# Loads and stores of two pairs issued as runs of four transfers

## The chip, the cores and the metric

One core of a Trainium2 chip. The metric is the device time of the whole kernel in microseconds (us); less is better. All comparisons here are between fast runs on one chip at a time. A ratio is the mean time of one kernel's fast runs over that of the kernel before in the same rounds, so it is not quite the ratio of the medians that stand beside it. Names of engines: PE is TensorE's matmuls and PEld its weight loads, DVE is VectorE, ACT ScalarE, POOL GpSimd; SP is SyncE, which here only issues transfers.

## The reference

`x` is [64, 1024, 1024] in fp32, 268 MB; the output has the same shape. Each token (row of 1024) goes to one of 16 heads, the one with the largest routing logit, and only that head's 64 columns of the output are not zero.

```python
route_logits = x @ route_w                      # [B, S, 16]
best_head = np.argmax(route_logits, axis=-1)
x_heads = x.reshape(B, S, 16, 64)
for h in range(16):
    out[:, :, h, :] = np.matmul(x_heads[:, :, h, :], experts[h]) * (best_head == h)[:, :, None]
```

## The kernel before

A *pair* is two tiles of 128 tokens, 1 MB of input and 1 MB of output; there are 256 pairs. A pair is loaded by two transfers of 512 KB (even and odd partitions) and stored by two. SP issues them all, on one queue, in the order load, load, store, store. Each transfer is spread over 16 DMA engines: four packets of 8 KB on each, then a write to a semaphore.

```python
WAYS = 2; XIN_BUFS = 10; OUT_BUFS = 6; XT_BUFS = 5; AHEAD = 7
ORDER = "TTTTFTFTFTTFTFTFTTTTTT"      # T: transpose on TensorE, F: matmul of a whole block

def load(g):
    xin = xin_pool.tile([P, 2, D], FP32, name="xin", tag="xin")
    for r in range(WAYS):
        nc.sync.dma_start(out=xin[r::WAYS], in_=xg[g, r::WAYS])
    return xin

def split_pass(xt):                   # five of eight blocks, in 64x64 parts of the array
    ps = ps_s_pool.tile([P, 2, HB], FP32, name="ps_s", tag="ps_s")
    for p in range(NS):
        ...
        for half in range(2):
            for th in range(2):
                nc.tensor.matmul(ps[th * 64:(th + 1) * 64, half, o0:o0 + W],
                    lhsT=xt[half * 64:(half + 1) * 64, p, th * 64:(th + 1) * 64],
                    rhs=mv[half * 64:(half + 1) * 64, p, :], ...)
    ...                               # ACT copies ps to raw, DVE sums logits

for j in range(-2 * AHEAD, NT + 2, 2):          # j: first tile of a pair
    if j + 2 * AHEAD < NT:
        xins[j + 2 * AHEAD] = load(j // 2 + AHEAD)
    if j < 0:
        continue
    pair = [i for i in (j - 2, j - 1) if i >= 0]
    for i in pair:
        work[i] = split_pass(xts[i])            # at the start of the pair's period
    ...                                         # then T of pair j, F of pair j-2, by ORDER
                finish(ot[:, i % 2, :], ps_w, *work.pop(i))   # argmax, mask; DVE and POOL write ot
                if i == pair[1]:
                    for r in range(WAYS):
                        nc.sync.dma_start(out=og[i // 2, r::WAYS], in_=ot[r::WAYS])
```

The split pass of a pair is recorded as 80 small matmuls and takes TensorE about 1.54 us of the 4.93 us that it needs for a pair.

## Time and profile before

| | before |
|---|---|
| time, median of 3 runs | 1341.66 us (1338.74 to 1343.21) |
| span of the profiled run | 1338.1 us |
| TensorE's period of a pair, median / mean | 4.926 / 5.136 us |
| one 8 KB packet, undisturbed | 309 ns |

The page of the kernel before: busy time of the compute engines, the busy share of the DMA engines and the data rate in forty slices of the span, the queue with its packets, MB and share of the 16 engines, and the chain of waits by engine and by line.

```profile
span 1338.1 us, 66342 instructions
...
PE 1290.3 (96%) x27648; PEld 1208.3 (90%) x27648; DVE 933.7 (70%) x4098; ACT 923.2 (69%) x1537; POOL 721.9 (54%) x1031
...
DMA  8999999999999999999999999999999999999997
GB/s 340 421 421 416 413 407 409 407 407 406 412 398 377 418 417 399 395 412 414 398 393 404 410 416 418 402 408 397 410 407 410 412 407 417 416 405 416 417 409 327
...
q1 hardware_dynamic: 81920, 536.94, 98.6%
...
HBM read 268.76 MB, written 268.44 MB: 401 GB/s over the span
...
DMA 96%; PE 1%; SPq 0%; DVE 0%; issue 0%; POOL 0%; ACT 0%; ACTq 0%; POOLq 0%; DVEq 0%
DMA out_dram<-ot 95%; DMA xin<-in_x_dram 1%; SPq L106 0%; PE ps_w L150 0%; PE ps_t L115 0%; DMA mv<-in_route_w_dram 0%; PE ps_s L136 0%; POOL ot L181 0%; DVE ot L173 0%; ACTq L88 0%; ACT raw L143 0%; ACT xt L117 0%; DVE mask L164 0%; POOLq L249 0%; DVE lg L158 0%
```

Nearly the whole span is filled by the one DMA queue, and the chain runs through stores. TensorE at 96% is close behind, which is why its pair period is worth reading: the median of 4.926 us is a pair without a wait, and the mean is 0.21 us longer.

Three stretches of the same run. Columns: stretch, its length, then busy us of each engine with its number of instructions, TensorE's granted clock, DMA share, GB/s.

```profile
core 0: us, PE busy (x) PEld busy (x) DVE busy (x) ACT busy (x) POOL busy (x), PEclk, DMA share, GB/s
600.00:650.00 50.00, 49.82 (x1083) 46.98 (x1083) 36.40 (x160) 36.04 (x61) 27.85 (x41) 1.00 1.01 411
650.00:700.00 50.00, 49.00 (x1077) 46.24 (x1076) 35.63 (x159) 35.32 (x60) 27.47 (x41) 1.00 1.00 392
1100.00:1200.00 100.00, 98.86 (x2142) 91.57 (x2141) 71.84 (x311) 70.29 (x118) 54.69 (x78) 1.00 1.01 412
```

The DMA share is 1.00 in all of them.

Who waits for whom, three lines of that view:

```profile
engine line waited for: us in total, times, longest us
...
DVE ot L173 <- DMA out_dram<-ot: 83.8, 104, 1.8
...
POOL ot L181 <- DMA out_dram<-ot: 76.3, 40, 3.0
...
PE ps_t L115 <- DMA xin<-in_x_dram: 6.9, 2, 6.6
```

Compute waits for stores to give back an output buffer, and hardly ever for a load. SP's own order of issues (start, duration, line, out<-in, count):

```profile
start us, us, engine line op out<-in xcount [idle before <-releaser]
602.66 0.50 SPq L223 DMA_DIRECT2D out_dram<-ot  x1
603.92 1.68 SPq L106 DMA_DIRECT2D xin<-in_x_dram  x2
606.49 1.77 SPq L223 DMA_DIRECT2D out_dram<-ot  x2
```

Each issue waits for the landing of the eighth transfer before, so eight are outstanding.

### The profile page before, as it was taken

How to read it: one execution, taken by the hardware profiler on the slowest of the kernel's cores; microseconds unless marked ns; L12 is line 12 of the kernel's file. 1: busy time of each engine (PE TensorE's matmuls, PEld its weight loads, DVE VectorE, ACT ScalarE, POOL GpSimd, SP SyncE). 2: the span in 40 equal slices, each digit the busy share in tenths (PEclk: the TensorE clock that was granted, in tenths of full speed). 3: DMA queues.
4: the chain of work that ended last, by engine and by line, in shares of the span. 5: the costliest groups of instructions: out<-in, count | busy, mean ns of one | idle time of the engine just before them, and what ended most of it. 6: DMA issues, size and time to landing. Idle time of an engine off the chain costs nothing.

```text
span 1338.1 us, 66342 instructions
## 1 busy us (share of the span) xinstructions
PE 1290.3 (96%) x27648; PEld 1208.3 (90%) x27648; DVE 933.7 (70%) x4098; ACT 923.2 (69%) x1537; POOL 721.9 (54%) x1031
## 2 busy tenths in 40 slices
PE   7999999999999999999999999999999999999995
PEld 7888998999998999999998999889998999999995
DVE  4666766677776777777777677667777777767775
ACT  5666766767766777777676776667766767767673
POOL 3455555555555555555555555555555555555554
PEclk9999999999999999999999999999999999999998
DMA  8999999999999999999999999999999999999997
GB/s 340 421 421 416 413 407 409 407 407 406 412 398 377 418 417 399 395 412 414 398 393 404 410 416 418 402 408 397 410 407 410 412 407 417 416 405 416 417 409 327
DMA packets 84412, 541.51 MB, mean 405 GB/s; under 512 B 18576, under 2 KB 18576, under 8 KB 18576
## 3 DMA queue, kind: packets, MB, share of 16 engines
q1 hardware_dynamic: 81920, 536.94, 98.6%
q8 instruction: 218, 3.57, 1.0%
q10 hardware_dynamic: 2192, 0.33, 0.1%
q14 instruction: 82, 0.67, 0.1%
HBM read 268.76 MB, written 268.44 MB: 401 GB/s over the span
## 4 chain that ended last, share of the span: by engine, by line
DMA 96%; PE 1%; SPq 0%; DVE 0%; issue 0%; POOL 0%; ACT 0%; ACTq 0%; POOLq 0%; DVEq 0%
DMA out_dram<-ot 95%; DMA xin<-in_x_dram 1%; SPq L106 0%; PE ps_w L150 0%; PE ps_t L115 0%; DMA mv<-in_route_w_dram 0%; PE ps_s L136 0%; POOL ot L181 0%; DVE ot L173 0%; ACTq L88 0%; ACT raw L143 0%; ACT xt L117 0%; DVE mask L164 0%; POOLq L249 0%; DVE lg L158 0%
## 5 line engine op out<-in xcount | busy, mean ns | idle before, releaser
L181 POOL TENSOR_TENSOR ot<-raw,mask 128x384 f32<-128x384 f32 (+1 forms) x1024 | 721.2, 725 | 605.6 <-ACT xt L117 338.0
L117 ACT COPY xt<-ps_t 128x512 f32<-128x512 f32 x1024 | 576.7, 589 | 288.5 <-PE ps_t L115 288.0
L115 PE MATMUL ps_t<-ident,xin 128*128 128x128 f32 x4096 | 756.5, 277 | 9.7 <-DMA xin<-in_x_dram 6.9
L150 PE MATMUL ps_w<-mf,xt 128*128 128x144 f32 x3072 | 580.3, 289 | 1.5 <-DVE ot L173 1.1
L115 PEld LDWEIGHTS ps_t<-ident,xin 128*128 128x128 f32 x4096 | 499.7, 141 | 33.6 <-issue 8.9
L150 PEld LDWEIGHTS ps_w<-mf,xt 128*128 128x128 f32 x3072 | 464.2, 191 | 8.8 <-DVE ot L173 6.3
L136 PE MATMUL ps_s<-mv,xt 64*64 64x80 f32 x20480 | 430.0, 232 | 22.6 <-issue 21.9
L136 PEld LDWEIGHTS ps_s<-mv,xt 64*64 64x64 f32 x20480 | 381.1, 133 | 73.2 <-issue 62.8
L143 ACT COPY raw<-ps_s 128x704 f32<-128x704 f32 x512 | 371.1, 747 | 104.3 <-PE ps_s L136 64.9
L173 DVE TENSOR_TENSOR ot<-ps_w,mask 128x384 f32<-128x384 f32 x512 | 285.6, 558 | 98.5 <-DMA out_dram<-ot 83.8
L127 DVE TENSOR_REDUCE lgs<-ps_s 128x16 f32<-128x96 f32 x512 | 121.4, 251 | 106.3 <-ACT raw L143 105.4
L164 DVE TENSOR_SCALAR mask<-hid,ix 128x16 f32<-128x16 f32 x512 | 120.0, 234 | 56.0 <-POOL ot L181 0.9
L124 DVE TENSOR_REDUCE lgw<-ps_w 128x16 f32<-128x48 f32 x512 | 103.3, 202 | 78.9 <-PE ps_w L150 78.1
L158 DVE TENSOR_TENSOR lg<-lgs,lgw 128x16 f32<-128x16 f32 x512 | 131.8, 257 | 17.6
L160 DVE MAX8 mx<-lg 128x8 f32<-128x16 f32 x512 | 91.2, 178 | 17.6
L162 DVE FIND_INDEX8 ix<-mx,lg 128x8 uint32<-128x16 f32 x512 | 86.5, 169 | 0.0
L162 DVE MATCH_VALUE_LOAD ix<-mx,lg 128x8 f32 x512 | 47.2, 92 | 17.7
L117 ACT ACT_TABLE_LOAD x1 | 1.3, 1283 | 7.3 <-DMA mf<-in_experts_dram 7.3
L81 DVE MEMSET mf<- 128x432 f32 x1 | 0.4, 418 | 0.9 <-PEq L238 0.9
masks.py:197 POOL MEMSET ident<- 128x128 f32 x1 | 0.2, 205 | 0.3 <-POOLq L238 0.3
masks.py:199 POOL TENSOR_SCALAR_AFFINE_SELECT ident<-ident 128x128 f32<-128x128 f32 x1 | 0.3, 294 | 0.0
L238 POOL MEMSET const-float32-0.0<- 128x1 f32 x1 | 0.1, 99 | 0.2 <-issue 0.2
(5 smaller groups left out, 0.6 us busy)
## 6 DMA issues: line engine op xcount, KB each, us to landing
xin<-in_x_dram SPq DMA_DIRECT2D x512, 512.0 KB, 10.2
out_dram<-ot SPq DMA_DIRECT2D x512, 512.0 KB, 10.2
mv<-in_experts_dram ACTq DMA_DIRECT2D x2, 48.0 KB, 4.7
mf<-in_experts_dram ACTq DMA_DIRECT2D x2, 48.0 KB, 2.4
mv<-in_experts_dram ACTq DMA_DIRECT2D x2, 32.0 KB, 3.9
mv<-in_route_w_dram ACTq DMA_DIRECT2D x1, 24.0 KB, 4.6
mf<-in_route_w_dram ACTq DMA_DIRECT2D x1, 24.0 KB, 3.1
mv<-in_route_w_dram ACTq DMA_DIRECT2D x1, 16.0 KB, 3.2
```

The source lines that it names most:

```text
L115: nc.tensor.transpose(ps_t[:, q, :], xin[:, t, p * P:(p + 1) * P], ident)
L117: nc.scalar.copy(out=xt[:, half * (NB // 2):(half + 1) * (NB // 2), :], in_=ps_t)
L124: nc.vector.tensor_reduce(out=lg, in_=parts.rearrange("k s h -> k h s"), op=ALU.add, axis=AX.X)
L127: nc.vector.tensor_reduce(out=lg, in_=parts.rearrange("k b s h -> k h b s"), op=ALU.add, axis=AX.XY)
L136: nc.tensor.matmul(ps[th * 64:(th + 1) * 64, half, o0:o0 + W], lhsT=xt[half * 64:(half + 1) * 64, p, th * 64:(th + 1) * 64], rhs=mv[half * ...
L143: nc.scalar.copy(out=raw[:, :, 0:RW], in_=ps[:, :, 0:RW])
L150: nc.tensor.matmul(ps[:, o0:o0 + STEP], lhsT=xt[:, NS + f, :], rhs=mf[:, f, :], start=(f == 0), stop=(f == NF - 1), skip_group_check=True)
L158: nc.vector.tensor_add(out=lg, in0=lgs, in1=lgw)
L162: nc.vector.max_index(out=ix, in_max=mx, in_values=lg)
L164: nc.vector.tensor_scalar(out=mask, in0=hid, scalar1=ix[:, 0:1], scalar2=None, op0=ALU.is_equal)
L173: nc.vector.tensor_tensor(out=ov[:, NS:], in1=bc(mk[:, NS:]), op=ALU.mult, in0=ps[:, W:W + NF * STEP].rearrange("k (f w) -> k f w", w=STEP ...
L181: nc.gpsimd.tensor_tensor(out=ov[:, ab:NS:2], in0=rv4[:, 0:n, :, o0:o0 + Dh], in1=bc(mk[:, ab:NS:2]), op=ALU.mult)
```

## The change

Its intent is to turn the direction of the memory traffic half as often: four loads (2 MB), then four stores (2 MB). A second pair is loaded with the first, the stores of the first pair wait for those of the second, one more output buffer is there for that, and the loads lead by 6 and 7 pairs instead of 7.

```diff
-OUT_BUFS = 6
+OUT_BUFS = 7
-AHEAD = 7
+AHEAD = 6
...
+    done = []
     for j in range(-2 * AHEAD, NT + 2, 2):
-        if j + 2 * AHEAD < NT:
-            xins[j + 2 * AHEAD] = load(j // 2 + AHEAD)
+        for i in (j + 2 * AHEAD, j + 2 * AHEAD + 2):
+            if j % 4 == 0 and i < NT:
+                xins[i] = load(i // 2)
...
                 if i == pair[1]:
-                    for r in range(WAYS):
-                        nc.sync.dma_start(out=og[i // 2, r::WAYS], in_=ot[r::WAYS])
+                    done.append((i // 2, ot))
+                if i == pair[1] and i % 4 == 3:
+                    for g, ot in done:
+                        for r in range(WAYS):
+                            nc.sync.dma_start(out=og[g, r::WAYS], in_=ot[r::WAYS])
+                    done = []
```

## The prediction

> **What bounds it now.** The DMA engines. The page's queue part gives the one queue that carries all loads and stores 98.6% of the 16 engines' span; stretches of 100 us show a DMA share of 1.00 to 1.01 at 402 to 418 GB/s. TensorE is only just behind: the starts of the split pass (80 matmuls, once a pair) lie 4.926 us apart at the median, with no wait, but 5.136 us in the mean. The difference, 255 x 0.21 = 54 us, is back-pressure: the waits view has DVE and POOL waiting 84 + 76 us for stores to free an output buffer. Without DMA limits it would take about 1285 us.
>
> **What the DMA time consists of (packet records).** An undisturbed 8 KB packet takes 309 ns, and the next begins 3 ns earlier; four of them and a semaphore write make 1.23 us for a transfer on one engine. 1024 x 1.23 = 1260 us. On top, per engine: packets longer than 309 ns, 45 us; instruction fetches (218 of 0.94 us over 16 engines), 13 us.
>
> Followed engine by engine, the 45 us are of two kinds.
> 1. First load packets after a switch of direction (those of both load transfers) are 30 to 55 ns too long in the mean, others about 3. They are long where the packet starts under 2 us after its issue, near none above 4 us: the engine has caught up with the issuing queue, which keeps only eight transfers outstanding (each issue waits for the landing of the eighth before).
> 2. One engine lags: after 150 us the sixteenth part of each transfer lands about 4 us after the fifteenth. Its store packets take about 329 instead of 309 ns; its loads are at 309. That is 8 x 20 = 160 ns a pair, 41 us in all. This engine sets the pace; kind 1 is the slack of the others. The Trainium skill, "DMA: Bandwidth & Descriptors", section "Latency and other measured facts", says engines 7 and 15 are usually slower; the trace agrees that one is, but doesn't number it.
>
> **What the change does.** Bytes, packets, compute: the same. Direction switches: halved (256 pairs of switches to 128). Issue i still waits for the eighth before, of its own kind. The first store of two is issued one pair (5 us) later; OUT_BUFS 7 pays for that. Lead of loads 6 to 7 pairs, far above the 10.2 us to landing. Last four stores instead of two wait for the last compute: about +2 us at the end.
>
> If all kind-1 stalls were critical, half of their 33 us, some 16 us, would be saved. Since the lagging engine sets the pace and hardly has them, I expect most of that not to arrive. What may change is its slow stores: it runs about four transfers behind the mean of the others, so now it stores while they store; in a period of eight it would store while they load. This may take away or add 10 to 20 us; I lean slightly to gain.
>
> **Predicted: 1332 us, 1306 to 1350.** Faster by over 2%: 0.18. Within 2%: 0.73. Slower by over 2%: 0.09.
>
> **Right if** DMA share stays at 1.00, mean GB/s within 1% or so of 405, the last part of each transfer still lands about 4 us late, its store packets stay near 329 ns, and PE's median period stays 4.926.
>
> **Wrong if** the stalls at switches do pace the kernel (then 1320 or less), if the slow stores vanish (about 1300), or if longer runs of stores slow all engines' writes, or the queue starves behind stores that wait for compute (gaps between packets, DMA share below 0.98; then 1360).

## The result, and the profile after

1360.57 us (1360.27 to 1361.66, 3 runs) against 1341.66: ratio 1.0146, 95% interval 1.0117 to 1.0175. The change is 19 us slower, clear of noise, and outside the predicted range. The page after, the same lines:

```profile
span 1358.5 us, 66340 instructions
...
PE 1298.0 (96%) x27648; PEld 1210.3 (89%) x27648; DVE 929.4 (68%) x4098; ACT 923.5 (68%) x1537; POOL 720.9 (53%) x1031
...
DMA  8999999999999999999999999999999999999997
GB/s 341 418 419 420 411 397 402 402 403 389 404 404 385 408 400 393 404 407 399 395 401 410 391 405 405 395 405 397 396 396 404 406 398 403 405 399 403 402 400 323
...
q1 hardware_dynamic: 81920, 536.94, 98.0%
...
HBM read 268.76 MB, written 268.44 MB: 395 GB/s over the span
...
DMA 58%; PE 39%; issue 1%; DVE 0%; POOL 0%; ACT 0%; SPq 0%; ACTq 0%; POOLq 0%; DVEq 0%
DMA out_dram<-ot 57%; PE ps_t L115 15%; PE ps_s L136 13%; PE ps_w L150 12%; DMA xin<-in_x_dram 1%; DMA mv<-in_experts_dram 0%; DVE ot L173 0%; POOL ot L181 0%; SPq L228 0%; ACT L117 0%; DVE ix L162 0%; DVE mask L164 0%; DVE lg L158 0%; DVE mx L160 0%; ACTq L88 0%
```

The same packets and bytes take 20 us more, at a queue share of 98.0%. The forty rates show the form of it: before, they swing between 377 and 421; after, none from the sixth on exceeds 410. The same stretches:

```profile
600.00:650.00 50.00, 48.74 (x1060) 44.51 (x1059) 33.71 (x148) 35.14 (x59) 26.07 (x37) 1.00 1.00 398
650.00:700.00 50.00, 48.71 (x996) 45.11 (x996) 35.46 (x158) 33.44 (x57) 27.39 (x40) 1.00 1.00 402
1100.00:1200.00 100.00, 97.56 (x2058) 90.00 (x2057) 69.72 (x305) 68.94 (x115) 53.30 (x76) 1.00 1.00 403
```

The DMA share is still 1.00, so the queue did not starve. Before, one stretch was fast and one slow; now both are in between. (The chain now passes through PE for 39%. With TensorE so close behind the DMA engines, the chain can follow either; a shift of its shares is no proof of a new limit, and TensorE's median pair period is still 4.926 us.) The waits and SP's issues:

```profile
engine line waited for: us in total, times, longest us
...
POOL ot L181 <- DMA out_dram<-ot: 174.2, 60, 4.0
...
DVE ot L173 <- DMA out_dram<-ot: 94.5, 60, 2.8
...
PE ps_t L115 <- DMA xin<-in_x_dram: 7.6, 3, 7.0
```

```profile
599.94 4.09 SPq L106 DMA_DIRECT2D xin<-in_x_dram  x4
604.95 4.70 SPq L228 DMA_DIRECT2D out_dram<-ot  x4
610.41 4.09 SPq L106 DMA_DIRECT2D xin<-in_x_dram  x4
```

POOL waits 98 us more for output buffers, which is back-pressure of slower stores: loads still keep nobody waiting.

### How the lagging engine is read

The prediction's claim that one DMA engine lags can be followed through. Each transfer raises its semaphore in 16 parts, one per engine. From about 150 us on the last part lands 3.8 us after the fifteenth in the kernel before (4.2 us after the change). The parts of this engine also have a delay of their own: they land about 450 ns (load) or 505 ns (store) after the packet record that raises them, the others' about 340 ns. That picks its packets out of the trace: by the count of that matching, all four could be followed for 806 of 839 transfers before, and for 746 after. Its time per transfer is the difference of two successive last landings, corrected for the two delays (middle part of the run, 15% to 96% of the transfers). These times need only the landings, not the followed packets.

| lagging engine, ns per transfer | load | store | overlap of a store with the split pass, us |
|---|---|---|---|
| before | 1253 | 1341 | 0.21 |
| after | 1240 | 1400 | 0.45 |

*Overlap* is how much of the time of a store transfer on this engine coincides with TensorE's split pass. The two changes give 512 x (1240 - 1253) = -6.7 us and 512 x (1400 - 1341) = +30.2 us, together +23.5 us; the spans differ by 20.4 us. So the place of the loss is found: the stores of the engine that lands last. The loads show the small gain that the change was made for.

### The profile page after: what moved, and what is told of

The parts are those of the page before. It is cut to its first block, busy times and chain, and to the rows that moved or that the text cites. A ratio compares the mean times of both kernels' runs of the same rounds, so it can differ in the third digit from the quotient of the medians.

```text
span 1358.5 us, 66340 instructions
## 1 busy us (share of the span) xinstructions
PE 1298.0 (96%) x27648; PEld 1210.3 (89%) x27648; DVE 929.4 (68%) x4098; ACT 923.5 (68%) x1537; POOL 720.9 (53%) x1031
## 4 chain that ended last, share of the span: by engine, by line
DMA 58%; PE 39%; issue 1%; DVE 0%; POOL 0%; ACT 0%; SPq 0%; ACTq 0%; POOLq 0%; DVEq 0%
DMA out_dram<-ot 57%; PE ps_t L115 15%; PE ps_s L136 13%; PE ps_w L150 12%; DMA xin<-in_x_dram 1%; DMA mv<-in_experts_dram 0%; DVE ot L173 0%; POOL ot L181 0%; SPq L228 0%; ACT L117 0%; DVE ix L162 0%; DVE mask L164 0%; DVE lg L158 0%; DVE mx L160 0%; ACTq L88 0%
## 5 line engine op out<-in xcount | busy, mean ns | idle before, releaser
L136 PE MATMUL ps_s<-mv,xt 64*64 64x80 f32 x20480 | 431.2, 233 | 23.9 <-issue 23.5
L158 DVE TENSOR_TENSOR lg<-lgs,lgw 128x16 f32<-128x16 f32 x512 | 124.0, 242 | 17.6
```

The costliest lines, as they stand in the source:

```text
L158: nc.vector.tensor_add(out=lg, in0=lgs, in1=lgw)
```

## The experiments

Four theories. **A1**: a long run of stores is slow on this engine. **A2**: its stores are slow while the other engines load, and the change shifts it against them. **B**: the changed readiness (stores held back, other buffer counts, shorter lead). **C**, formed after the first four runs: its stores are slow while TensorE runs the split pass; before, the rhythm of transfers and that of the pair were equal and kept the two apart.

### First: the parts of the change, and other lengths of run

`sizes`: the kernel before with two numbers changed.

```diff
-OUT_BUFS = 6
+OUT_BUFS = 7
-AHEAD = 7
+AHEAD = 6
```

> The kernel before with OUT_BUFS 7 and AHEAD 6 alone, transfers still alternating by pair. Theory A (order of transfers slows the stores of the one lagging DMA engine): same as before, ratio 0.998 to 1.002, last-landing interval of the store transfers about 1345 to 1390 ns as before. Theory B (the shorter lead of loads or another buffer count costs): slower, up to 1360 us.

Measured: 1346.41 us against 1341.50, ratio 1.006 (0.998 to 1.014), no difference that the runs can tell. The four runs scatter, though: 1338 and 1339, but also 1353 and 1355 us. Only the one of 1339 was profiled: lagging engine 1247 and 1342 ns, overlap 0.18, as before. So the sizes do not by themselves bring the change's stores of 1400 ns; what the two long runs did is not known.

`run4`, `run1`, `run8`: a store is issued when its pair is ready, and after every RUN stores RUN loads are issued; 18 loads at the start, OUT_BUFS 7.

```diff
+for _ in range(18):
+    load_next()
-for j in range(-2 * AHEAD, NT + 2, 2):
+for j in range(0, NT + 2, 2):
...
                         nc.sync.dma_start(out=og[i // 2, r::WAYS], in_=ot[r::WAYS])
+                        at["store"] += 1
+                        if at["store"] % RUN == 0:
+                            for _ in range(RUN):
+                                load_next()
```

> Same order of transfers in the queue as the change (four loads, four stores) but each store is issued as soon as its pair is ready, not one pair later; loads primed to 18 as before. Theory A (order of transfers): 1356 to 1364 us, lagging engine's stores 1360 to 1490 ns apart. Theory B (stores held back one pair, compute stalls on output buffers): back to about 1340 us.

Measured: 1362.12 us, ratio 1.0163 (1.0112 to 1.0214), the change's time without its held-back stores and with a longer lead. With `sizes`, B falls. Lagging engine 1234 and 1408 ns, overlap 0.44.

> Single transfers alternate, load, store, load, store. Theory A1 (a long run of stores is slow for the lagging engine): faster than before, 1320 to 1338 us. Theory A2 (a store is slow on the lagging engine while the other engines load; with single transfers they are always mixed): about 1335 to 1350. Switching theory (each change of direction costs time on the engine that sets the pace): slower than before, over 1350.

Measured: 1359.37 us, ratio 1.0143 (1.0093 to 1.0194): slower, so A1 alone falls, and A2's range is missed. The forecast of the switching theory, over 1350, was met. Lagging engine 1289 and 1342 ns, overlap 0.32. So here the whole loss is in the loads: 36 ns each, or 18 us in 512. Every load now follows a store, and the first packet of such a load takes 323 ns in the mean, against 309 for a load that follows a load; that explains part of it, the rest stays open. No run alternates single transfers without compute, so that a turn at every transfer costs time is neither shown nor excluded. The case below concerns runs of two and four.

> Runs of eight loads and eight stores, stores issued as soon as ready. Theory A1 (length of the run): slower still than the change, 1370 or more, all store positions from the third on slow. Theory A2 (state of the other engines; the lagging engine is four to five transfers behind): about as the change, 1350 to 1365, with the first four stores of a run near 1330 ns and the last four near 1450. Theory B: much slower, over 1380, DMA share under 1.

Measured: 1368.54 us, ratio 1.0202 (1.0151 to 1.0252). Lagging engine 1234 and 1406 ns, overlap 0.43. The last-landing intervals of the eight stores of a run (ns, not corrected for the delays):

```
1343  1524  1435  1378  1377  1528  1387  1326
```

Neither A1 (rising) nor A2 (low, then high) looks like that. There are two peaks, four transfers apart, and four transfers are about as long as TensorE's period of a pair. That led to C. The mean overlap with the split pass at the same eight places (us) has the same two peaks:

```
0.01  0.98  0.60  0.10  0.32  0.98  0.33  0.07
```

The four places of a run in `after` agree (0.19, 0.55, 0.79, 0.24 us of overlap; 1368, 1435, 1487, 1364 ns, uncorrected too). These are right kernels; a pattern that comes again after four, within a run of eight, is not one of the place in the run alone.

Sorted by when they run, the lagging engine's packets point the same way (mean ns of a packet; only those with no instruction fetch in flight on any engine):

| | store, no split pass | store, in the split pass | load, no split pass | load, in the split pass |
|---|---|---|---|---|
| before | 323 | 357 | 313 | 314 |
| after | 322 | 383 | 311 | 310 |

With a fetch in flight the stores in the split pass take 369 and 378, much the same, so TensorE's instruction traffic is not the cause. The column of stores in the split pass depends on how packets are picked: a second matching, which loses more of the disturbed stores, gave 330 and 338 there, and the other columns within 3 ns.

The fit over whole transfers needs no picking: over the store transfers of a run (those under 2000 ns), the time is 1295 to 1311 ns plus 204 to 228 ns per us of overlap in `before`, `sizes`, `after`, `run4` and `run8` (1273 plus 221 in `run1`). The kernel before holds its own control: for stores that end from 600 to 650 us the mean overlap is 0.16 us (0.03 up to 637 us, where the rhythm slips), from 650 to 700 us it is 0.67, and these are the stretches of 411 and 392 GB/s shown above. After the change it is 0.42 and 0.38 there, at 398 and 402 GB/s. By chance alone one would expect about 1.54 / 5.1 of a store's 1.4 us, 0.42 us.

### Second: attempts to take the split pass away or move it

`cut2` and `cut4` replace the split pass by large matmuls, in runs of two and of four. They, and below `trans2`, `trans4`, `dma2`, `dma4`, `quad4`, `quad2` and `splitdma`, issue as `run4` does, with RUN 2 or 4. No run issues in this way in runs of two and keeps the kernel's compute; the kernel before stands in for it.

```diff
-        for p in range(NS):
-            ...                                  # the small matmuls
+        for half in range(2):
+            nc.tensor.matmul(ps[:, half, 0:RL], lhsT=xt[:, half, :],
+                rhs=mf.rearrange("k f w -> k (f w)")[:, 0:RL], start=True, stop=True, ...)
```

> Wrong result on purpose: the 80 small matmuls of the split pass (1.54 us a pair) are replaced by four large ones; transfers in runs of two. Theory C (a store packet of the one lagging DMA engine is slow while TensorE runs the split pass; read from the first traces: about 1300 ns a store transfer plus 220 ns per us of overlap): the stores of that engine come down to 1300 to 1320 ns, time 1305 to 1330 us. Theories A1 and A2 (order of transfers alone, whatever TensorE does): the stores stay at 1340, time about 1340 us.

> The same with runs of four loads and four stores. Theory C: as cut2 within 5 us (the 20 us between the two orders vanish). Theories A1 and A2: 15 to 25 us slower than cut2, stores of the lagging engine near 1400 ns.

Measured: 1482.56 and 1481.82 us. A miss of mine: the large matmuls take 2.64 us a pair, TensorE is 99% busy and becomes the limit, so the order of transfers can't show.

`halves2` moves the second tile's split pass to the middle of the pair.

```diff
-        for i in pair:
+        for i in pair[:1]:
             work[i] = split_pass(xts[i])
...
             f += 1
+            if f == NF:
+                work[pair[1]] = split_pass(xts[pair[1]])
```

> Order of transfers as before (runs of two); the split pass of the second tile of the pair is moved on TensorE from the start of the pair to its middle, so the small matmuls lie at two places of the pair period. Right result. Theory C: they can no longer all lie beside the loads; mean overlap with a store rises from 0.2 to 0.3 to 0.45 us and the time by 8 to 25 us, to 1350 to 1366 us. Theories A1 and A2: no change, 1340 us, unless TensorE itself waits more (then its median pair period rises above 4.93 us).

Measured: 1393.67 us, ratio 1.0388 (1.0360 to 1.0416), but the median pair period rose to 5.338 us and the chain is TensorE's:

```profile
DMA  8999999999999999999999999999999999999984
...
PE 98%; DVE 1%; ACT 0%; DMA 0%; issue 0%; POOL 0%; POOLq 0%; ACTq 0%; DVEq 0%
```

Void as a test of C: slower for a reason of its own.

`x15` tries to name the lagging engine: one store in twelve is cut into 60 rows and 4 rows.

```diff
+                        if r == 1 and (i // 2) % 6 == 5:
+                            nc.sync.dma_start(out=og[i // 2, 1:121:2], in_=ot[1:121:2])
+                            nc.sync.dma_start(out=og[i // 2, 121:128:2], in_=ot[121:128:2])
+                        else: ...                # as before
```

> The kernel before, but one store transfer in twelve is split into 60 rows (divisible by 15: fifteen engines) and 4 rows, so the sixteenth engine has 53 us less to move. If the sixteenth engine is the one that lags, theory 'one engine sets the pace' expects about 1290 to 1320 us and the lag of the last part of a transfer near 0; if another engine lags, 1340 us and the lag stays near 4 us.

Measured: 1362.83 us, ratio 1.0153 (1.0121 to 1.0185). In the stretch from 600 to 640 us the last part of whole transfers still lands 2.6 us in the mean behind the one before it. The cut stores say more. A store of 60 rows shows fifteen landings, and from 100 to 750 us (21 of them) the last of the fifteen is 1.1 to 4.4 us late, within 0.3 us of the transfer before: the lagging engine is one of these fifteen. A store of 4 rows shows four landings, and all four come before that late part: it is none of these four. By the Trainium skill ("DMA: Bandwidth & Descriptors", section "Why a DMA increments its semaphore by 16 and not by 1"), 60 rows go to the lowest-numbered fifteen engines. If so, the sixteenth is not the one that lags; the count of fifteen agrees with the trace, but no run here checks that numbering. Why this version is slower was not looked into.

### Third: the split pass replaced at equal time, and no compute at all

`trans2` and `trans4` replace the split pass by twelve transposes a pair, about 1.4 us.

```diff
-        for p in range(NS):
-            ...                                  # the small matmuls
+        for half in range(2):
+            for o in range(3):
+                nc.tensor.transpose(ps[:, half, o * P:(o + 1) * P], xt[:, 3 * half + o, :], ident)
```

> Wrong result on purpose: the 80 small matmuls of the split pass are replaced by 12 transposes of 128x128 a pair, about 1.4 us, so TensorE has nearly the same time a pair (about 4.8 us) but no 64-row work; transfers in runs of two, OUT_BUFS 7. Theory C (stores of the lagging engine are slow during the split pass): its store transfers 1290 to 1310 ns, no dependence on the overlap with this stretch (under 50 ns per us instead of 220), time 1308 to 1325 us. Theories A1 and A2 (order alone): stores 1340, time about 1338 us.

> The same with runs of four. Theory C: within 5 us of trans2. Theories A1 and A2: 15 to 25 us above trans2, with the lagging engine's stores near 1400 ns.

Measured: `trans2` 1312.86 us, ratio 0.9798 (0.9767 to 0.9829); `trans4` 1321.95 us, ratio 0.9867 (0.9835 to 0.9898). Lines of the pages of `trans2` and then `trans4`: span, rates in forty slices, and the queue of instruction fetches.

```profile
span 1311.1 us, 31522 instructions
...
GB/s 339 424 423 423 424 420 414 417 413 411 418 417 409 414 419 408 417 418 414 409 417 418 399 420 418 410 416 412 417 409 417 419 409 415 414 413 416 416 409 335
...
q8 instruction: 82, 1.34, 0.4%
```

```profile
span 1320.0 us, 31522 instructions
...
GB/s 343 419 423 424 424 421 414 413 417 400 414 412 408 414 407 413 413 410 416 399 414 416 405 409 420 405 411 414 410 403 418 411 405 413 408 412 413 411 413 328
...
q8 instruction: 82, 1.34, 0.4%
```

The time falls, and the gap between the orders shrinks from about 20 us to 9. The stores of the lagging engine take 1291 and 1327 ns. In `trans4` they depend on the overlap with the transposes by 26 ns per us, where it was 212 in `run4`: it is the split pass, not the stretch of time, that hurts. Plainer still, stores that met this stretch for over 1.2 us took 1626 ns in the mean in `run4` (73 stores) and 1344 in `trans4` (98), and those that missed it 1315 and 1314.

Two limits: stores that miss it are slower in both than without compute (1229, below), so other compute disturbs them too; and the transposes are not free. In `trans2` no store meets them for more than 0.5 us; over all its stores the slope is -140 ns per us, as the second stores never meet them and are slower (1313 against 1269), but among the first stores alone it is +162.

Part of the fall is not C's: 136 fewer instruction fetches of 0.94 us are worth 8 us, in both alike (an estimate, with the fetches spread evenly over 16 engines, which the trace does not number). Theory C's "within 5 us" was missed: with transposes in its place a smaller effect of the same kind is left. In `trans2` the first store of each pair falls where its packets are almost undisturbed (1252 ns, the second 1294), while in `trans4` three of four take 1303 to 1325 (means of the transfers whose packets could be followed; the range covers both matchings). Which of the remaining compute does that was not separated.

`dma2` and `dma4` drop all compute and store one tile of zeros, in runs of two and of four.

```diff
-    for j in range(-2 * AHEAD, NT + 2, 2):
-        ...                                      # the loads as issued before, and all compute
+    ot = out_pool.tile([P, 2, D], FP32, name="ot", tag="ot")
+    nc.vector.memset(ot, 0.0)
+    for g in range(NT // 2):
+        ...                                      # the stores of pair g; after each RUN stores, RUN loads
```

> No compute at all (zeros are stored, wrong on purpose); the same 512 loads and 512 stores in runs of two. Theory C: lagging engine's stores near 1240 to 1290 ns in dma2 and dma4 alike, 1275 to 1310 us. Rival: 1330 us or more here too, as the engine's slowness then needs no compute.

> As dma2 in runs of four. Theory C: within 5 us of dma2 (a few us faster if switches of direction cost anything). Theories A1 and A2: some 20 us slower than dma2.

Measured: 1274.28 and 1275.76 us, ratios 0.9512 (0.9482 to 0.9543) and 0.9522 (0.9492 to 0.9553). Totals and queue of `dma2` and then `dma4`:

```profile
DMA packets 84120, 537.33 MB, mean 422 GB/s; under 512 B 18576, under 2 KB 18576, under 8 KB 18576
...
q1 hardware_dynamic: 81920, 536.94, 100.3%
```

```profile
DMA packets 84120, 537.33 MB, mean 422 GB/s; under 512 B 18576, under 2 KB 18576, under 8 KB 18576
...
q1 hardware_dynamic: 81920, 536.94, 100.3%
```

The order of transfers by itself, in runs of two or four, costs nothing and saves nothing (1.5 us apart): A1 and A2 fall, and so does the change's own idea. The engine that lands last does 1236 ns a load and 1229 a store (1237 and 1228 in `dma4`), as fast as the 309 ns packets allow. So no engine is slow without compute; one is slowed beside it. The 422 GB/s agree with the Trainium skill, "HBM Reference", section "Specifications (TRN2)", which gives about 425 GB/s for a core that streams alone.

### Fourth: moving the rhythm in a right kernel

`flast` and `ffirst` change only ORDER; `out4` only the output buffers.

```diff
-ORDER = "TTTTFTFTFTTFTFTFTTTTTT"
+ORDER = "TTTTTTTTTTFTFTFTTFTFTF"     # flast
+ORDER = "FTFTFTTFTFTFTTTTTTTTTT"     # ffirst
-OUT_BUFS = 6
+OUT_BUFS = 4                         # out4
```

> Kernel before, but the six whole-block matmuls of a pair come after its sixteen transposes on TensorE instead of among them, so the output is finished nearer to the next split pass; transfers unchanged, runs of two. Theory C: the overlap of stores with the split pass changes, and the time follows it: 1340 us plus 0.11 us for each ns of mean overlap above 210 ns (220 ns per us x 512 stores), e.g. 1365 at 0.45 us, 1325 at 0.08 us; which way is not foreseen, a guess is lower overlap. Order theory: 1340 us unless TensorE's own median period rises.

> The same with the six whole-block matmuls first, right after the split pass (alternating with six transposes and ten transposes last). Theory C: time follows the measured overlap by the same rule; a guess is higher overlap than before, 0.3 to 0.5 us, 1350 to 1370 us. Order theory: 1340 us unless TensorE's own median period rises.

Measured: 1451.46 and 1434.80 us. Both void: the median pair period rose to 5.551 and 5.431 us. The chain of `flast`, no DMA in it:

```profile
DMA  9999999999999999999999999999999999999984
...
ACT 31%; PE 28%; POOL 21%; issue 17%; DVE 1%; ACTq 0%; DMA 0%; POOLq 0%; DVEq 0%
```

> Kernel before with four output buffers instead of six. Theory C: TensorE is held closer to the landings of the stores, slips of the rhythm are shorter, mean overlap under 0.21 us, 1320 to 1340 us; if the queue now starves behind stores that aren't ready, slower, with DMA share under 1.0.

Measured: 1337.83 us against 1337.64, ratio 1.0005 (0.9954 to 1.0056). Overlap fell to 0.14 us, stores to 1327 ns, loads 1252; the gain that this should bring, about 8 us, is within the scatter of the kernel before (1332 to 1345). In the profiled run part of it was lost at the end: the last of the forty slices moved 268 GB/s instead of 327. Neither confirmed nor refuted.

`quad4` and `quad2` let TensorE work on two pairs at a time, so that its rhythm fits runs of four and no longer runs of two.

```diff
-XT_BUFS = 5
+XT_BUFS = 9
-ORDER = "TTTTFTFTFTTFTFTFTTTTTT"
+ORDER = "SSTTTTTTSSFTFTFTTFTFTFTTTTTTTTFTFTFTTFTFTFTTTTTT"    # S: split pass of one tile
-    for j in range(-2 * AHEAD, NT + 2, 2):
+    for j in range(0, NT + 4, 4):
...                                          # issue as in run4, RUN 4 or 2
```

> Right result. Runs of four as in the change (stores issued when ready), TensorE works on two pairs at a time: split passes of four tiles within about 4 us, then the rest. Theory C (coincidence with the split pass): the four passes fall in the half period in which the lagging engine loads; mean overlap under 0.25 us per store transfer, time 1325 to 1345 us, against 1362 of run4. Order theories: as run4, 1360. Void if TensorE's own time for two pairs rises over 10.2 us.

> The same TensorE order with runs of two. Theory C: the passes now span loads and stores, overlap 0.35 to 0.5 us, time 1350 to 1365 us, slower than quad4. Order theories: as before, 1340, faster than quad4. Void if TensorE's own time for two pairs rises over 10.2 us.

Measured: 1506.23 and 1478.99 us. Void: TensorE stalls (73 us before split-pass matmuls and 38 us before whole-block ones in `quad4`), two pairs take 11.6 and 11.4 us, and the limit is compute.

### Last: the suspect alone

`splitdma` is `dma2` with the split-pass matmuls of all 512 tiles added on a constant input, and nothing else.

```diff
+    xt = xt_pool.tile([P, NB, P], FP32, name="xt", tag="xt")
+    nc.vector.memset(xt, 0.5)
+    for _ in range(NT):
+        split_pass(xt)               # its copies and sums taken out
```

> Zeros are stored, wrong on purpose. Theory C: while the split passes run (first 400 us), the lagging engine's store transfers take 1450 to 1600 ns and its loads 1230 to 1250; after they end, both 1230 to 1260 as in dma2. Time 1310 to 1345 us (dma2 1274, plus 0.6 us a pair over some 70 pairs, plus instruction fetches). Rival (the slowness needs ACT, DVE and POOL): stores below 1300 ns in both stretches, time below 1295 us.

Measured: 1328.21 us, 54 us more than `dma2`'s 1274.28 (measured on another occasion; both had about 1340 beside them). Rows of its page:

```profile
PE   4555656565555566565665566565000000000000
...
PEclk8777787887788877878777777778555555555555
DMA  8999999999999999999999999999999999999998
GB/s 339 422 422 422 413 410 410 400 403 392 411 391 391 392 410 414 393 412 408 396 399 403 406 410 401 399 404 406 403 425 427 427 426 421 426 427 426 427 423 351
```

Stretches (order of columns as above, without ACT):

```profile
250.00:350.00 100.00, 61.44 (x2304) 58.21 (x2304) 0.00 (x0) 0.00 (x0) 0.78 1.01 401
650.00:750.00 100.00, 57.12 (x2156) 53.90 (x2152) 0.00 (x0) 0.00 (x0) 0.77 1.00 401
1000.00:1100.00 100.00, 0.00 (x0) 0.00 (x0) 0.00 (x0) 0.00 (x0) 0.50 1.01 426
```

(PEclk, the granted clock, is near 0.77 while the matmuls run, against 1.00 in the kernel before, so they are not quite paced as there.) TensorE runs to about 930 us, at 57 to 61% busy rather than back to back, so longer than the 400 us that I expected and with less overlap. In the first 130 us the rate is still 422 GB/s: the last part is only 0.7 us behind (50 to 150 us), which fits the reading that one engine is slow and holds up the others only when it has fallen back far enough. From 250 us to the end of the matmuls the rate is near 401 GB/s, and the lagging engine takes 1241 ns a load and 1388 a store, with the last part 4.0 us behind. After it ends, the rate is 426 GB/s at once, 1240 a load and 1225 a store. Loads are untouched, stores lose 163 ns each; at a duty near 0.58, a 1.39 us store overlaps by some 0.8 us, so about 200 ns per us of overlap; fitted transfer by transfer it is 181. That is close to the slope in the full kernels. No ACT work, and no DVE or POOL work in that stretch, is there, so the rival falls. Instruction fetches still run beside the matmuls, but the stores with none in flight (166 of 286) are no faster, 1415 ns. The size of 1450 to 1600 that I gave assumed a full overlap (the 129 stores that overlapped by more than 1.2 us took 1475); that the time fell in the range I gave is luck, as the matmuls ran more than twice as long and slowed each store less.

No version beat the kernel before with a right result; `trans2` is faster but wrong.

## Why the prediction was wrong

Right, and shown: the DMA engines set the time; one engine sets their pace; the held-back stores cost nothing (`run4`), and the sizes nothing that was found (`sizes`); TensorE's median stayed at 4.926 us; the DMA share stayed at 1.00; the last part still lands about 4 us late; the saving on turns of direction did not arrive. The gain on the lagging engine's loads was 13 ns each, 6.7 us in all.

Wrong is the step "What may change is its slow stores: it runs about four transfers behind the mean of the others, so now it stores while they store; in a period of eight it would store while they load", with its "lean slightly to gain". I took the 20 ns excess of its store packets for a matter between DMA engines, and so for something that might go either way by 10 to 20 us. That 20 us is near what was measured is luck, as it was reckoned from another mechanism. So is the 1360 us in the "wrong if" part: the causes named with it, slow writes of all engines or a queue that starves, are not what happened (`dma4` is not slowed, the DMA share stayed at 1.00). The runs show in place of that step that:

- without compute that engine is not slow in either order (`dma2`, `dma4`: 1229 and 1228 ns a store), so it was not the other engines' direction;
- the split pass alone makes its stores slow and leaves its loads alone (`splitdma`: 1388 against 1225 ns a store, 1241 against 1240 a load); of two stretches of about equal length on TensorE, the split pass hurts far more than transposes (`run4` and `trans4`: 212 and 26 ns per us within each run; against a store without compute, 1229 ns, a store that meets the stretch for over 1.2 us loses 397 and 115 ns);
- before, the stores mostly fell outside the split pass (0.21 us of overlap a store, 0.03 in its best stretches), as both rhythms had the period of a pair; runs of four have the period of two pairs, one half of the stores meets the split pass (the second and third of each four, see above), and the overlap went to 0.45 us. 512 stores x 0.23 us x 220 ns per us is 26 us of the 30 us that the stores lost.

The mean rate fell to 399 GB/s, more than the 1% that I allowed. A smaller error: "its store packets stay near 329 ns". They had two levels, 323 outside the split pass and more in it (357 in the table above), and 329 was the blend. I had not asked the trace what TensorE did while they ran.

What is not shown: the causal runs (`trans4`, `dma4`, `splitdma`) are not right kernels; of the attempts to shift the rhythm in a right kernel, `out4` moved it too little to tell and the others made compute the limit. In right kernels the link rests on the fit, the places in a run and the stretches of the kernel before. That the kernel before keeps its rhythm because TensorE waits for output buffers is argued from the waits. Why one engine suffers more than the others, where the store meets the split pass, why the loads of `run1` are slow, and what causes the remaining 9 us between `trans2` and `trans4`, stays open.

## What to carry to other kernels

When a DMA queue is always busy and its rate still differs from stretch to stretch, sort the packets by what the compute engines do at that time and by direction, before explaining them by other transfers. If loads, stores and compute share one period, their phases may keep to each other, as they mostly did here, and a change of grouping on one side can give that up even when it costs nothing by itself. Test an order of transfers without compute first: here two runs (`dma2`, `dma4`) settled that the idea had nothing to gain.

## What the Trainium skill lacked or had wrong

- "SBUF — State Buffer", section "SBUF: two separate sides", says "A DMA cannot be slowed by a compute op, and vice versa." Here stores on the engine that lands last went from 1225 to 1388 ns a transfer, and the stream from 426 to 401 GB/s, while nothing but small TensorE matmuls and their instruction fetches ran beside them (`splitdma`); its loads stayed at 1240 ns. Where in the path the two meet was not found, so this does not say that they meet at the SBUF ports.
- "DMA: Bandwidth & Descriptors", section "Latency and other measured facts", calls engines 7 and 15 usually slower. The page's best guess at the cause is for SWDGE transfers, those issued from POOL; here SP issued every load and store. One engine did lag, by 3.8 us, but the lag grew only beside compute: without it, it did 1229 ns a store, full rate (`dma2`). The trace does not number it; it was one of the fifteen that took 60 rows and none of the four that took 4 (`x15`).
- No page says what a change of direction costs. Without compute, runs of two and of four transfers of 512 KB took 1274.28 and 1275.76 us. Turns at every transfer were run only beside compute (`run1`: 1359.37 us).
- No page says that, in a queue with eight transfers outstanding and one slow engine, the other engines' waits can look like long packets. The prediction read 30 to 55 ns too much on first packets of loads, about 3 on others; from 250 to 900 us the mean 8 KB packet of all engines took 321.7 ns in the kernel before and 309.0 without compute (`dma2`).
